# Inverse square roots of the norms: one power instruction on GpSimd in place of eleven Newton instructions on VectorE

## The chip, the cores and the metric

One core of a Trainium2 chip runs the whole program. The metric is device time in microseconds (us), taken as the median of repeated runs. The engines are called by the names of the profile: PE (TensorE, the matrix engine; PEld is its weight load), DVE (VectorE), ACT (ScalarE), POOL (GpSimd) and SP (SyncE, which issues the DMAs).

## What is computed

Two blocks of two layers each, over 512 tokens of width 1024, in float32. The first block mixes attention (with 256 context tokens beside the 512), a 31-wide depthwise convolution and a pooling branch, then a gated feed-forward part. The second block mixes a low-rank latent attention (MLA) with a gated linear attention (GLA) and adds a per-layer embedding. What matters here is that every norm needs the inverse square root of a mean over channels, one number per token and head:

```python
def rms_norm(t, g):
    ms = jnp.mean(jnp.square(tf), axis=-1, keepdims=True)
    return (tf * lax.rsqrt(ms + RMS_EPS)).astype(t.dtype) * g
def layer_norm(t, g, b):
    return ((tf - mu) * lax.rsqrt(var + LN_EPS)).astype(t.dtype) * g + b
```

## The kernel before, in words

Every matrix product is made of three: weights and activations are split into a high and a low part, and high x high, high x low and low x high are accumulated. Weights come in pieces of 128 x 1024 by SP's queue, ACT rounds a piece to the high part (line 178) and DVE subtracts to get the low part (line 181); nearly all PE work is `mm` (line 186).

No order of instructions is written out by hand for the engines. The program is written in source order, with priorities for some stretches, and a planner that simulates a timeline by its own costs orders each engine's instructions; each engine then runs its list in that order. The list mixes instructions of parts that do not depend on each other.

Forty inverse square roots are taken, all by `rsqrt` (lines 203 to 215). Tokens lie on the 128 partitions, so a root has only 2 to 12 columns. From a bit trick as the first guess (lines 209 and 210), three Newton rounds follow, of three DVE instructions each (lines 212, 213, 214): eleven small instructions, each of which needs the one before. The input is made on DVE by one affine instruction (mean and epsilon). The callers:

- `inv_rms` (20 roots): squares on ACT, column sums on PE, the sums turned onto the partitions by small products, then the affine line 264 out of PSUM, then `rsqrt`. It serves `ln` (the convolution's layer norm, and both layer norms of `out_ffn`, by segment), `norm_in` (the input norms of the second block, half the tokens at a time) and `final`. The result goes to PE, which multiplies it with the identity to broadcast it along the partitions (`bcast_cols`); what is scaled by the norm, on DVE or ACT, comes after.
- `kv` (4 roots, 6 columns): line 434, then `rsqrt`; ACT then scales the keys (line 439) before they are transposed.
- `qtrans` (8 roots, 8 or 12 columns): line 479, `rsqrt`, and line 482, which folds in the attention scale. Its result is used per query tile in `softmax`, by a small DVE multiply and by ACT's exponential.
- `lowrank_scale` (4 roots): lines 1194 to 1197 make the input, `rsqrt`, then a product (line 1200). The second of each pair is broadcast by PE for the keys of the MLA (line 1502 uses it).
- `gla` (4 roots, 8 columns): line 1466, `rsqrt`, then ACT (1472) and DVE (1474) scale the outputs before they are transposed.

Beside them on DVE: the 31 taps of the convolution (line 593) in the attention stages; the last affine lines of the norms (281, 283, 1019). On POOL: the rope's products and table multiplies (370, 388, 395, 397), the pooling windows and their edges (632 to 646), rescaling of the residual (808, 809, 1005, 1006, 1023, 1308), and the GLA's gate subtraction and fills (1342, 1354, 1355, 1361, 1368, 1391). The scratch tiles of the roots come from a ring of 24 of 16 columns.

Of the kernel before, what the change touches and what calls it, by code (L numbers as in the profile page):

```python
# [10 lines left out]
F32 = mybir.dt.float32  # L11
F32R = mybir.dt.float32r
I32 = mybir.dt.int32
U32 = mybir.dt.uint32
AF = mybir.ActivationFunctionType
ALU = mybir.AluOpType
# [4 lines left out]
P = 128  # L21
# [9 lines left out]
RMS_EPS = 1e-6  # L31
ALPHA = (2 * DEPTH) ** 0.25
WINDOWS = (2, 4, 8, 16)
ATTN_SCALE = 128 ** -0.5
# [25 lines left out]
class W:  # L60


    def __init__(self, pieces, kp, mc):
        self.pieces, self.kp, self.mc = pieces, kp, mc
# [13 lines left out]
class Net:  # L78
# [15 lines left out]
    def __init__(self, es, tc, a):  # L94
        self.es, self.tc, self.nc, self.a = es, tc, tc.nc, a
        nc = self.nc
        self.n_w, self.npt, self.nps = 0, 0, 0
        self.cst = es.enter_context(tc.tile_pool(name="cst", bufs=1))
        self.wp = es.enter_context(tc.tile_pool(name="wp", bufs=1))
        self.xp = es.enter_context(tc.tile_pool(name="xp", bufs=1))  # L100
        self.dr = es.enter_context(tc.tile_pool(name="dr", bufs=1, space=DRAM))
        self.uid = 0
        self.cols2 = []
        for l in range(DEPTH):
            t = self.cst.tile([P, NCOL2], F32, name=f"cols2{l}")
            nc.sync.dma_start(t, a["cols2"][l])
            self.cols2.append(t)
        self.fin = self.cst.tile([P, 8], F32, name="fin")
        nc.sync.dma_start(self.fin, a["final_norm"])
        c = self.cst  # L110
        self.ident = c.tile([P, P], F32, name="ident")
        make_identity(nc, self.ident)
        self.ones = c.tile([P, P], F32, name="ones")
        nc.vector.memset(self.ones, 1.0)
        self.cmean = c.tile([P, P], F32, name="cmean")
        nc.vector.memset(self.cmean, 1.0 / 32)

# [82 lines left out]
                self.mm(ps[:m1 - m0, c0:c0 + n], wl, xh[:, c0:c0 + n], False, last)  # L200


    def rsqrt(self, x, n, out=None):

        v = self.nc.vector
        i = self.S(n, I32)
        y = self.S(n) if out is None else out
        t = self.S(n)
        v.tensor_scalar(i, x.bitcast(I32), 1, None, op0=ALU.logical_shift_right)
        v.tensor_scalar(y.bitcast(I32), i, -1, 0x5F3759DF, op0=ALU.mult, op1=ALU.add)  # L210
        for _ in range(3):
            v.tensor_tensor(t, y, y, ALU.mult)  # L212
            v.scalar_tensor_tensor(t, t, -0.5, x, ALU.mult, ALU.mult)
            v.scalar_tensor_tensor(y, t, 1.5, y, ALU.add, ALU.mult)
        return y

    def bcast_cols(self, ps, r, nt):

        for t in range(nt):
            self.mm(ps[:, t * P:(t + 1) * P], r[:, t:t + 1].broadcast_to([P, P]), self.ident, True, True)  # L220
# [190 lines left out]
    def kv(self, l, j, toks, out):  # L411

        nc = self.nc
        tab = self.table(l, 1)
        w = self.wload(self.a["w_in"][l, CH_KV + j], KT, 256)
        brow = self.c1.tile([P, 256], F32, tag="brow", bufs=2, name=self.nm("brow"))
        nc.sync.dma_start(brow[:, :P], self.a["b_rows"][l:l + 1, 1024 + j * P:1024 + (j + 1) * P].broadcast_to([P, P]))
        vh, vl = self.al("KV", F32R), self.al("KV", F32R)
        kh, kl = self.al("KV", F32R), self.al("KV", F32R)
        ss = self.S(6)  # L420
        os = []
        for tp in range(3):
            ps = self.ps("pp")
            self.tok_proj(ps, w, *toks[tp])
            pv = ps[:, :512].rearrange("p (t h d) -> p t h d", t=2, h=2)
            vv = pv[:, :, 1, :]
            dst = slice(2 * tp * P, (2 * tp + 2) * P)
            hv = vh[:, dst].rearrange("p (t d) -> p t d", t=2)
            nc.scalar.copy(hv, vv)
            nc.vector.tensor_tensor(vl[:, dst].rearrange("p (t d) -> p t d", t=2), vv, hv.bitcast(F32), ALU.subtract)  # L430
            os.append(self.norm_rope(ps, pv[:, :, 0:1, :], brow[:, :P], 1, tp, tab, ss[:, 2 * tp:2 * tp + 2]))
            yield
        x = self.S(6)
        nc.vector.tensor_scalar(x, ss, 1.0 / 128, RMS_EPS, op0=ALU.mult, op1=ALU.add)
        r = self.rsqrt(x, 6)
        for tp in range(3):
            o = os[tp]
            for i in range(2):
                nc.scalar.activation(o[:, i * P:(i + 1) * P], o[:, i * P:(i + 1) * P], AF.Copy, scale=r[:, 2 * tp + i:2 * tp + i + 1])
            pt = self.ps("pt")  # L440
            for i in range(2):
                nc.tensor.transpose(pt[:, i * P:(i + 1) * P], o[:, i * P:(i + 1) * P], self.ident)
            self.split(kh[:, tp * 256:tp * 256 + 256], kl[:, tp * 256:tp * 256 + 256], pt[:, :256])
        out["kv", j] = kh, kl, vh, vl
        yield
# [18 lines left out]
    def qtrans(self, os, ss):  # L464

        nc = self.nc
        qs = []
        for o in os:
            pt = self.ps("pt")
            for t in range(2):  # L470
                for h in range(2):
                    nc.tensor.transpose(pt[:, h * 256 + t * P:h * 256 + (t + 1) * P],
                                        o[:, (t * 2 + h) * P:(t * 2 + h + 1) * P], self.ident)
            qh, ql = self.al("Q", F32R)[:, :SEQ], self.al("Q", F32R)[:, :SEQ]
            self.split(qh, ql, pt[:, :512])
            qs.append((qh, ql))
        n = 4 * len(os)
        x = self.S(12)
        nc.vector.tensor_scalar(x[:, :n], ss[:, :n], 1.0 / 128, RMS_EPS, op0=ALU.mult, op1=ALU.add)
        r = self.rsqrt(x[:, :n], n)  # L480
        sc = self.S(12)
        nc.vector.tensor_scalar(sc[:, :n], r, ATTN_SCALE, None, op0=ALU.mult)
        return qs, sc

    def softmax(self, ps, n, sc, out):

# [830 lines left out]
    def gla(self, l, j, q, k, sm, gv, md):  # L1317

        nc = self.nc
        v, s, g = nc.vector, nc.scalar, nc.gpsimd  # L1320
# [102 lines left out]
        ss = self.S(8)  # L1423
# [3 lines left out]
        for t in range(4):  # L1427
# [34 lines left out]
            s.copy(og[:, t * 256:(t + 1) * 256], po[:, :256])  # L1462
            for hh in range(2):
                s.activation(junk[:, :P], po[:, hh * P:(hh + 1) * P], AF.Square, accum_out=ss[:, 2 * t + hh:2 * t + hh + 1])
        x = self.S(8)
        v.tensor_scalar(x, ss, 1.0 / P, RMS_EPS, op0=ALU.mult, op1=ALU.add)
        r = self.rsqrt(x, 8)
        for hh in range(2):
            for t in range(4):
                o = og[:, t * 256 + hh * P:t * 256 + (hh + 1) * P]  # L1470
# [239 lines left out]
```

## Time and profile before

| what | value |
|---|---|
| median of 3 runs | 3476.34 us (3474.51 to 3477.19) |
| the profiled execution's own time | 3477.77 us |
| its span | 3476.0 us |
| mean granted TensorE clock | 0.961 |
| PE busy | 94% of the span |
| DVE busy | 64% |
| ACT busy | 40% |
| POOL busy | 15%, 581 instructions |

The profile shows one execution. Its span runs from the first to the last instruction; the execution's own time has a little around it. Busy time is that of the instructions alone, without the waiting before them. A line number is a line of the kernel; several callers can share the line of a helper such as 186 or 212. Where an instruction stood idle first, the profile names what ended the wait.

### The profile page before, as it was taken

What the parts mean: (1) busy time and instruction counts of PE and PEld (TensorE: products, weight loads), DVE (VectorE), ACT (ScalarE), POOL (GpSimd) and SP (SyncE); (2) the same over time, 40 slices, a digit from 0 to 9 for tenths busy, and PEclk for the clock granted to TensorE, in tenths of its full rate; (3) what the DMA queues carried; (4) which work ended last, traced back from release to release, by engine and by line L of the source; (5) the groups of instructions that cost most, each with busy time, mean ns of one, the idle gap of its engine ahead of it and who ended that gap; (6) DMA issues with size and microseconds to landing.
All of it is one profiled execution on the core that took longest, in us unless ns stands there. A gap on an engine that the chain in (4) does not pass through costs nothing.

```text
span 3476.0 us, 47198 instructions
## 1 busy us (share of the span) xinstructions
PE 3252.7 (94%) x18622; PEld 2680.6 (77%) x18622; DVE 2215.7 (64%) x3623; ACT 1381.4 (40%) x2362; POOL 528.7 (15%) x581
## 2 busy tenths in 40 slices
PE   7999999899999999999999989999998979998897
PEld 4887787778778888877888857788877757886586
DVE  5795968744554444457988956654555675657655
ACT  2434343433332112233544434432335545554453
POOL 2120212222120000003111204200001220112101
PEclk8999999999999999998999999999999989999899
DMA  6232312233333432232222234433333222442223
GB/s 250 67 117 88 120 56 70 68 98 93 102 122 128 140 122 64 58 106 82 76 66 85 88 99 131 122 96 97 97 115 107 90 68 85 148 155 86 79 87 108
DMA packets 110909, 350.80 MB, mean 101 GB/s; under 512 B 12832, under 2 KB 19424, under 8 KB 105568
## 3 DMA queue, kind: packets, MB, share of 16 engines
q1 hardware_dynamic: 110688, 347.79, 31.5%
q8 instruction: 146, 2.39, 0.3%
q14 instruction: 75, 0.61, 0.1%
HBM read 326.77 MB, written 20.97 MB: 100 GB/s over the span
## 4 chain that ended last, share of the span: by engine, by line
PE 71%; DVE 13%; ACT 3%; issue 2%; POOL 1%; DMA 0%; POOLq 0%; DVEq 0%; SPq 0%; ACTq 0%
PE pp L186 59%; DVE W L593 5%; PE st L186 3%; PE ps L186 3%; PE pv L186 2%; DVE wl L181 1%; PE pt L186 1%; DVE T L287 1%; DVE s L489 1%; ACT wh L178 0%; DVE M L287 0%; PE pt L527 0%; PE gb L1457 0%; DVE s L212 0%; ACT M L286 0%
## 5 line engine op out<-in xcount | busy, mean ns | idle before, releaser
L181 DVE TENSOR_TENSOR wl<-wr,wh 128x1024 fp32r<-128x1024 f32 (+2 forms) x482 | 589.5, 1226 | 353.7 <-ACT wh L178 351.5
L178 ACT CAST wh<-wr 128x1024 fp32r<-128x1024 f32 (+2 forms) x482 | 490.8, 1021 | 768.8 <-PE pp L186 701.1
L186 PE MATMUL pp<-A,wh 128*128 128x512 f32 (+1 forms) x3392 | 774.6, 343 | 17.8 <-ACT A L286 7.9
L186 PE MATMUL pp<-C,wh 128*128 128x512 f32 (+1 forms) x2328 | 658.5, 368 | 31.6 <-DVE M L1212 18.5
L186 PEld LDWEIGHTS pp<-A,wh 128*128 128x128 f32 x3392 | 537.7, 191 | 128.7 <-issue 25.1
L186 PEld LDWEIGHTS pp<-C,wh 128*128 128x128 f32 x2328 | 415.8, 192 | 123.0 <-issue 35.1
L186 PE MATMUL pp<-A,wl 128*128 128x512 f32 (+1 forms) x1696 | 460.4, 340 | 0.0
L186 PE MATMUL pp<-C,wl 128*128 128x512 f32 (+1 forms) x1164 | 424.9, 366 | 0.0
L186 PE MATMUL pp<-B,wh 128*128 128x512 f32 (+1 forms) x1296 | 315.9, 350 | 0.0
L186 PE MATMUL pp<-M,wh 128*128 128x256 f32 (+1 forms) x1280 | 293.8, 324 | 12.9 <-ACT M L1114 4.5
L186 PEld LDWEIGHTS pp<-A,wl 128*128 128x128 f32 x1696 | 271.9, 190 | 39.4 <-issue 4.7
L593 DVE SCALAR_TENSOR_TENSOR W<-W,cw,W 128x783 f32<-128x783 f32 x240 | 269.2, 1125 | 2.1
L186 PEld LDWEIGHTS pp<-C,wl 128*128 128x128 f32 x1164 | 223.0, 192 | 44.2 <-issue 8.6
L186 PEld LDWEIGHTS pp<-M,wh 128*128 128x128 f32 x1280 | 214.6, 194 | 43.3 <-issue 14.1
L186 PEld LDWEIGHTS pp<-B,wh 128*128 128x128 f32 x1296 | 212.1, 188 | 37.8 <-issue 2.9
L186 PE MATMUL pp<-M,wl 128*128 128x256 f32 (+1 forms) x640 | 205.8, 322 | 0.0
L186 PE MATMUL pp<-B,wl 128*128 128x512 f32 (+1 forms) x648 | 193.5, 349 | 0.0
L593 DVE SCALAR_TENSOR_TENSOR W<-U,cw,W 128x512 f32<-128x512 f32 x240 | 189.2, 789 | 3.0
L866 DVE SCALAR_TENSOR_TENSOR B<-pp,cols,B 128x511 f32<-128x511 f32 x66 | 43.4, 658 | 211.6 <-ACT B L863 211.4
L831 DVE SCALAR_TENSOR_TENSOR X<-pp,g,X 128x512 f32<-128x512 f32 (+1 forms) x128 | 76.9, 630 | 156.2 <-PE pp L186 155.9
L863 ACT ACTIVATE B<-pp,cols 128x768 f32<-128x768 f32 (+1 forms) x44 | 38.9, 885 | 232.9 <-PE pp L186 232.9
L186 PEld LDWEIGHTS pp<-M,wl 128*128 128x128 f32 x640 | 124.3, 194 | 9.2 <-issue 2.0
(398 smaller groups left out, 4938.5 us busy)
## 6 DMA issues: line engine op xcount, KB each, us to landing
wr<-w_in SPq DMA_DIRECT2D x184, 512.0 KB, 3.8
wr<-w_up SPq DMA_DIRECT2D x96, 512.0 KB, 3.8
wa<-w_ada SPq DMA_DIRECT2D x40, 1024.0 KB, 5.0
wr<-w_out SPq DMA_DIRECT2D x64, 512.0 KB, 3.9
wr<-w_down SPq DMA_DIRECT2D x48, 512.0 KB, 3.6
wr<-w_ple_gate SPq DMA_DIRECT2D x32, 512.0 KB, 4.1
Z<-w_ada SPq DMA_DIRECT2D x16, 512.0 KB, 8.5
wr<-conv_pw SPq DMA_DIRECT2D x16, 512.0 KB, 3.8
```

The costliest lines, as they stand in the source:

```text
L178: nc.scalar.copy(hi[:, :n], raw[:, :n])
L181: eng.tensor_tensor(lo[:, :n], raw[:, :n], hi[:, :n].bitcast(F32), ALU.subtract)
L186: self.nc.tensor.matmul(out, l, r, start=start, stop=stop)
L287: self.nc.vector.tensor_tensor(lo, t, hi.bitcast(F32), ALU.subtract)
L489: nc.vector.tensor_reduce(nm, ps[:, :n], AX.X, ALU.max, negate=True)
L593: nc.vector.scalar_tensor_tensor(y, gl[:, i:i + no], ws[:, i:i + 1], y, ALU.mult, ALU.add)
L831: nc.vector.scalar_tensor_tensor(xs[t][:, c0:c0 + sn], ps[:, c0:c0 + sn], g5[:, t, q:q + 1], xs[t][:, c0:c0 + sn], ALU.mult, ALU.add)
L863: nc.scalar.activation(y[:, :n], pa[:, :n], AF.Identity, bias=self.col(l, "fdw_b")[:, f:f + 1], scale=cw[:, 1:2])
L866: nc.vector.scalar_tensor_tensor(y[:, c0 + 1:e], pa[:, c0:e - 1], cw[:, 0:1], y[:, c0 + 1:e], ALU.mult, ALU.add)
```

## The change

`rsqrt` becomes one `tensor_tensor` power on POOL, with a constant tile of -0.5 as the exponent, and where a scale is asked for, one POOL multiply behind it. A new helper `rms_scale` also makes the input on POOL (mean and epsilon), for `kv`, `qtrans` and `gla`. `inv_rms` and `lowrank_scale` make their input on DVE as before and only the root moves. The constant is filled by DVE once, at the start.

```diff
--- before.py
+++ after.py
@@ -112,6 +112,8 @@
         make_identity(nc, self.ident)
         self.ones = c.tile([P, P], F32, name="ones")
         nc.vector.memset(self.ones, 1.0)
+        self.nhalf = c.tile([P, 16], F32, name="nhalf")
+        nc.vector.memset(self.nhalf, -0.5)
         self.cmean = c.tile([P, P], F32, name="cmean")
         nc.vector.memset(self.cmean, 1.0 / 32)
 
@@ -200,19 +202,19 @@
                 self.mm(ps[:m1 - m0, c0:c0 + n], wl, xh[:, c0:c0 + n], False, last)
 
 
-    def rsqrt(self, x, n, out=None):
-
-        v = self.nc.vector
-        i = self.S(n, I32)
+    def rsqrt(self, x, n, out=None, scale=1.0):
+
         y = self.S(n) if out is None else out
-        t = self.S(n)
-        v.tensor_scalar(i, x.bitcast(I32), 1, None, op0=ALU.logical_shift_right)
-        v.tensor_scalar(y.bitcast(I32), i, -1, 0x5F3759DF, op0=ALU.mult, op1=ALU.add)
-        for _ in range(3):
-            v.tensor_tensor(t, y, y, ALU.mult)
-            v.scalar_tensor_tensor(t, t, -0.5, x, ALU.mult, ALU.mult)
-            v.scalar_tensor_tensor(y, t, 1.5, y, ALU.add, ALU.mult)
+        self.nc.gpsimd.tensor_tensor(y, x, self.nhalf[:, :n], ALU.pow)
+        if scale != 1.0:
+            self.nc.gpsimd.tensor_scalar(y, y, scale, None, op0=ALU.mult)
         return y
+
+    def rms_scale(self, ss, n, d, scale=1.0):
+
+        x = self.S(n)
+        self.nc.gpsimd.tensor_scalar(x, ss[:, :n], 1.0 / d, RMS_EPS, op0=ALU.mult, op1=ALU.add)
+        return self.rsqrt(x, n, None, scale)
 
     def bcast_cols(self, ps, r, nt):
 
@@ -430,9 +432,7 @@
             nc.vector.tensor_tensor(vl[:, dst].rearrange("p (t d) -> p t d", t=2), vv, hv.bitcast(F32), ALU.subtract)
             os.append(self.norm_rope(ps, pv[:, :, 0:1, :], brow[:, :P], 1, tp, tab, ss[:, 2 * tp:2 * tp + 2]))
             yield
-        x = self.S(6)
-        nc.vector.tensor_scalar(x, ss, 1.0 / 128, RMS_EPS, op0=ALU.mult, op1=ALU.add)
-        r = self.rsqrt(x, 6)
+        r = self.rms_scale(ss, 6, 128)
         for tp in range(3):
             o = os[tp]
             for i in range(2):
@@ -475,12 +475,7 @@
             self.split(qh, ql, pt[:, :512])
             qs.append((qh, ql))
         n = 4 * len(os)
-        x = self.S(12)
-        nc.vector.tensor_scalar(x[:, :n], ss[:, :n], 1.0 / 128, RMS_EPS, op0=ALU.mult, op1=ALU.add)
-        r = self.rsqrt(x[:, :n], n)
-        sc = self.S(12)
-        nc.vector.tensor_scalar(sc[:, :n], r, ATTN_SCALE, None, op0=ALU.mult)
-        return qs, sc
+        return qs, self.rms_scale(ss, n, 128, ATTN_SCALE)
 
     def softmax(self, ps, n, sc, out):
 
@@ -1462,9 +1457,7 @@
             s.copy(og[:, t * 256:(t + 1) * 256], po[:, :256])
             for hh in range(2):
                 s.activation(junk[:, :P], po[:, hh * P:(hh + 1) * P], AF.Square, accum_out=ss[:, 2 * t + hh:2 * t + hh + 1])
-        x = self.S(8)
-        v.tensor_scalar(x, ss, 1.0 / P, RMS_EPS, op0=ALU.mult, op1=ALU.add)
-        r = self.rsqrt(x, 8)
+        r = self.rms_scale(ss, 8, P)
         for hh in range(2):
             for t in range(4):
                 o = og[:, t * 256 + hh * P:t * 256 + (hh + 1) * P]
```

## Rows read from the trace of the kernel before

**Rows 1.** The page: span; busy time, share of it and instructions of each engine.

```profile
span 3476.0 us, 47198 instructions
...
PE 3252.7 (94%) x18622; PEld 2680.6 (77%) x18622; DVE 2215.7 (64%) x3623; ACT 1381.4 (40%) x2362; POOL 528.7 (15%) x581
```

**Rows 2.** Stretch, its length; busy PE, PEld, DVE, ACT, POOL; PEclk, DMA, GB/s.

```profile
1600.00:1830.00 230.00, 219.75 (x1303) 192.04 (x1303) 202.00 (x344) 109.22 (x223) 38.02 (x46) 0.99 0.25 76
2785.00:2830.00 45.00, 29.22 (x127) 20.65 (x127) 36.98 (x77) 14.02 (x27) 19.14 (x19) 0.70 0.15 50
```

**Rows 3.** Line L212: count, ns (min/median/max), first and last start, shapes.

```profile
L212 DVE TENSOR_TENSOR s<-s x120: 149/161/1233, 92.0 to 3467.3; 128x2 f32<-128x2 f32 x48, 128x8 f32<-128x8 f32 x24, 128x4 f32<-128x4 f32 x21, 128x6 f32<-128x6 f32 x15
```

**Rows 4.** Timeline: start, us, engine, line, operation [idle before <- releaser].

```profile
968.63 0.16 DVE L264 TENSOR_SCALAR s<-st 128x2 f32<-128x2 f32 x1 [4.40 <-PE st L186]
...
970.79 0.16 DVE L214 SCALAR_TENSOR_TENSOR s<-s,s 128x2 f32<-128x2 f32 x1
...
971.10 0.55 PE L186 MATMUL st<-ident,s 128*128 128x128 f32 x1 [2.51 <-DVE s L214]
```

**Rows 5.** What PE waited for: us in total, times, the longest.

```profile
PE pt L186 <- DVE s L214: 11.0, 5, 2.8
PE st L186 <- DVE s L214: 10.9, 3, 4.7
```

**Rows 6.** Timeline of all engines, from three stretches with an exposed root.

```profile
1563.42 0.16 DVE L264 TENSOR_SCALAR s<-st 128x2 f32<-128x2 f32 x1 [3.21 <-PE st L186]
...
1568.53 0.58 PE L186 MATMUL pt<-ident,s 128*128 128x128 f32 x1 [2.82 <-DVE s L214]
...
2227.91 0.16 DVE L264 TENSOR_SCALAR s<-st 128x2 f32<-128x2 f32 x1 [3.33 <-PE st L186]
...
2231.52 0.55 PE L186 MATMUL st<-ident,s 128*128 128x128 f32 x1 [3.65 <-DVE s L214]
...
2610.99 0.16 DVE L264 TENSOR_SCALAR s<-st 128x2 f32<-128x2 f32 x1 [1.96 <-PE st L186]
...
2612.26 3.21 DVE L1019 SCALAR_TENSOR_TENSOR X<-X,cols,st 128x256 f32<-128x256 f32 x8
...
2616.65 1.23 PE L186 MATMUL st<-ident,s 128*128 128x128 f32 x4 [4.73 <-DVE s L214]
2617.99 0.48 DVE L1019 SCALAR_TENSOR_TENSOR X<-X,cols,st 128x256 f32<-128x256 f32 x1 [1.40 <-PE st L186]
```

**Rows 7.** POOL's groups by shape: busy us, mean ns | idle before.

```profile
L644 POOL TENSOR_TENSOR W<-W,edge 128x1 f32<-128x1 f32 x4 | 3.0, 772 | 0.0
...
L646 POOL TENSOR_TENSOR W<-W,edge 128x1 f32<-128x1 f32 x4 | 0.8, 192 | 0.0
```

**Rows 8.** Timeline, POOL's table multiplies beside a root's second step.

```profile
1563.20 3.70 POOL L370 TENSOR_TENSOR T<-T,grow 128x512 f32<-128x512 f32 x3 [0.86 <-DMA T<-rope_cos]
...
1564.52 1.19 DVE L210 TENSOR_SCALAR s<-s 128x2 int32<-128x2 int32 x1
```

**Rows 9.** Timeline of the gap in the first layer of block 2.

```profile
2787.70 0.34 DVE L1197 TENSOR_SCALAR s<-s 128x4 f32<-128x4 f32 x1
...
2788.04 0.52 POOL L1355 MEMSET G<- 64x512 f32 x1
...
2789.91 2.54 POOL L1342 TENSOR_TENSOR L<-L,G 128x512 f32<-128x512 f32 x2 [1.35 <-DVE L L1331]
...
2790.34 0.89 DVE L209 TENSOR_SCALAR s<-s 128x4 int32<-128x4 int32 x1
...
2807.94 0.16 DVE L1200 TENSOR_TENSOR s<-s,s 128x4 f32<-128x4 f32 x1
...
2808.25 0.55 PE L186 MATMUL pv<-ident,s 128*128 128x128 f32 x1 [3.15 <-DVE s L1384]
```

**Rows 10.** DVE's timeline in the second layer's attention: ends of one `qtrans` root.

```profile
1693.22 0.70 DVE L479 TENSOR_SCALAR s<-s 128x8 f32<-128x8 f32 x1
...
1711.45 0.16 DVE L482 TENSOR_SCALAR s<-s 128x8 f32<-128x8 f32 x1
```

## The prediction

> **What bounds the kernel now.** I read the page's busy shares first: TensorE (PE) is busy 3252.7 us of 3476.0, VectorE (DVE) 2215.7, GpSimd (POOL) only 528.7 [rows 1]. So the end moves only where PE stands still, or where another engine is saturated and PE starves behind it. The table by stretch shows where that is [rows 2]. In the attention of the second layer (1600 to 1830) DVE is busy 202.00 of 230.00 us. In the 45 us from 2785 DVE is busy 36.98 and PE only 29.22, at a mean granted clock of 0.70: a gap in which PE waits for a string of short steps.
>
> Next I read the Newton lines. L212 stands for all: three of it per root, 120 in all, so 40 roots; its median is 161 ns and its longest 1233 ns [rows 3]. By the code the 40 roots are 20 from `inv_rms`, 4 from `lowrank_scale`, 4 from `kv`, 8 from `qtrans` and 4 from `gla`. Where DVE has nothing else to do, a root looks like the one at 968 us [rows 4]: the input line L264 starts at 968.63, the last L214 starts at 970.79, and PE's broadcast of the root starts at 971.10, after standing 2.51 us. That is 2.47 us from input to consumer: eleven dependent steps 0.20 apart and a hop of about 0.15 to PE (970.79 + 0.16 to 971.10). The list of PE's waits shows how often it matters: L214 released PE eight times, for 11.0 and 10.9 us [rows 5]. Seven of the eight are long; the eighth, 0.5 us, is left at nothing.
>
> **Part one: the exposed roots.** Six more roots look like that one [rows 6]. The list pairs input and broadcast of 1563.42 and 1568.53, of 2227.91 and 2231.52, and of 2610.99 and 2616.65; the roots that enter at 3022.70, 3435.37 and 3465.55 repeat the 2.47 of [rows 4], PE standing 2.51, 2.71 and 2.51. With the change the path is L264 (0.16), a hop to POOL, the power, and a hop to PE. I take 0.2 for both hops, an estimate a little over the one of 0.15 above, and call the power p: p + 0.35 in place of 2.47.
>
> The trace has no power on POOL, so p is bounded by POOL's smallest multiplies: 0.19 us for a 128x1 one that met nothing, 0.77 for one that shared the time with DVE's convolution [rows 7]. The low end is 0.19. For the high end I let the power cost eleven of the dear multiplies, 8.5 us, as if POOL did Newton's work itself. I take p = 1.0: a power is more than one multiply, and the widths are 2 to 12 columns, so I go somewhat over the dear row it is nearest to.
>
> At p = 1.0 the path is 1.35. The four plain roots save 1.1 each, 4.4. The one at 2227.91 saves 3.61 - 1.35 = 2.3. For the one at 2610.99 the reader behind it (L1019 of the second segment, at 2617.99) comes after eight L1019 of the first segment (3.21 us from 2612.26), which end at 2615.5; it can't start earlier, so 2.5 is saved and not 4.3 [rows 6]. At 1563 POOL runs three table multiplies for 3.70 us from 1563.20 [rows 8]; the power stands before them or behind, so I take half of 5.11 - 1.35: 1.9. Sum: 11.1 us, and it falls by 7 for each us more of p.
>
> **Part two: the gap in each layer of the second block.** The second `lowrank_scale` enters DVE at 2787.70 and its product L1200 ends at 2808.10; PE's broadcast of it starts at 2808.25 after standing 3.15 us [rows 9] (the profile names L1384, a fill behind L1200, but the operand is L1200's). In between the planner has strewn the eleven steps among the GLA's work, and DVE never rests. The eleven add up to 4.56 us, since some last far over the median: the L209 takes 0.89 [rows 9], and the L212 at 2806.28 is the longest of all, 1.23 [rows 3]. All eleven become POOL's one instruction. POOL is free from the end of a fill at 2788.56 to the gate subtraction at 2789.91 [rows 9], so at p = 1.0 the power fits in front of it. If p is longer, that subtraction, the scan behind it on DVE and the whole GLA wait; that is the cover, and it costs p less 1.0 if gone. Saved: 3.5 a layer, leaving one for port waits; the second layer repeats it at 3196 to 3216. Sum 7.0, falling by 2 per us of p.
>
> **Part three: the twelve roots of the attention stages** (`kv` four times, `qtrans` eight). Here DVE's order mixes the steps with convolution taps: one `qtrans` root runs from 1693.22 to 1711.61 [rows 10]. Mixed so, a step costs DVE about 0.1 us, some 1.3 us a root with the two affine lines. In exchange POOL gets two instructions per `kv` root and three per `qtrans` root, 32 in all: the affine one, the power and the scale. At 0.75 for each small one and 1.0 for a power that is 4 x 1.75 + 8 x 2.5 = 27 us of POOL.
>
> How much of it stalls DVE is read from [rows 8]: an L210 of two columns that began beside POOL's three table multiplies lasted 1.19 us, about the length of one of the three, where a step takes 0.16 when POOL rests [rows 4]. So a DVE step can wait for a whole POOL instruction. Not every DVE line will meet one, so I take half of the 27 as stalls: 12 x 1.3 - 13.5 = +2, of which I book nothing, as the attention doesn't end on DVE alone. The bounds are +16 (no stall) and 16 - 27 = -11 (all of it). Per us of p it loses 12 x 0.5 = 6.
>
> [...]
>
> Behind a waiting affine line on POOL stand the rope multiplies and the pooling windows; who waits for the result is ScalarE's scaling of the keys and, new, the softmax's small multiply on DVE.
>
> **Part four, at nothing.** The other roots, thirteen of `inv_rms` and the first of each `lowrank_scale` pair, have PE's other products beside them: [rows 5] has no wait for them. If that cover were gone each would cost or save its own p + 0.35 against 2.47. The four roots of the GLA outputs feed ScalarE and DVE ahead of the transposes, and release PE nowhere in [rows 5]. The constant is one DVE fill before the first L212 at 92.0 us [rows 3]. Fewer scratch tiles rotate; no DMA is added or moved, so SP's queue has nothing new ahead of it.
>
> **Sum.** 11.1 + 7.0 + 0 = 18 us. The profiled execution took 3477.77, its span 3476.0 with 1.8 around it, 1.4 above the median of 3476.34. Taken off the median: 3458. The rate over all parts is 7 + 2 + 6 = 15 us per us of p, so the gain is gone at p = 2.2.
>
> [...]
>
> **Rivals.** First, **slower: the power is dear.** [...] It decides at p = 2.2. At p = 3 the time is 3476 + 12 = 3488, at 4 us 3503, at the bound of 8.5 us 3571. For it: POOL does nothing like a power here, and its 128x1 multiply can take 0.77. Against it: three multiplies of 512 columns take POOL 3.70 us together [rows 8], and here there are 12 columns at most. Chance 0.21.
>
> [...] Chance 0.07.
>
> Third, **the gain is given back.** Behind an exposed root comes ScalarE's copy or split and then weights that wait anyway, and the planner orders every engine anew, with shifts of a few us either way. For it: the root at 2610.99, half covered by L1019. Against: PE has no matmul between input and broadcast in the seven. Time 3472 to 3480. Chance 0.09.
>
> Fourth, **the change does not do what it says**: the power is queued behind long POOL work, so that a wait for POOL takes the place of eleven steps. Time about 3476; chance 0.03, since of the seven only the one at 1563 has POOL work between input and broadcast.
>
> **How the numbers follow.** Forecast 0.60, rivals 0.21, 0.07, 0.09 and 0.03. What a measurement can tell from no change is about 0.2%, 7 us: 3469 to 3483. The forecast lies below that (p under 1.5), the first rival above, the others within or at its edge: faster 0.60, same 0.19, slower 0.21. The predicted time is the forecast's, 3458. The range's low end is p = 0.19: 18 + 15 x 0.8 = 30 us, 3446. The high end is the first rival at p = 3, 3488; what is beyond, up to 3571, and a re-plan better than the low end hold less than 0.2.
>
> **What would show it.** Right: a POOL power of about 1 us; 1.3 us from L264 to the broadcast at the seven places; no long Newton line in the gap, and that gap 3 to 4 us shorter; DVE less busy by the 440 steps, some 70 us at their median. Wrong: powers over 2.2 us, convolution taps (L593) longer than before beside them, PE's waits moved from L214 to POOL at the same length, or a time that falls outside the places named.

## The result: 3438 us, and the profile after

The changed kernel takes **3438.45 us** (median of 4 runs, 3434.70 to 3442.10), the kernel before beside it 3475.43 (4 runs): a ratio of 0.9898, 95% interval 0.9879 to 0.9917. The direction was forecast, the size was not: 18 us were predicted and 35.5 came (1.02% of 3475), and 3438 lies below the range of 3446 to 3488. The profiled execution took 3437.51.

The page of the kernel after, its span and its busy times by engine, to set against [rows 1]:

```profile
span 3435.7 us, 46787 instructions
...
PE 3238.6 (94%) x18622; PEld 2670.4 (78%) x18622; DVE 2152.9 (63%) x3160; ACT 1380.5 (40%) x2362; POOL 597.1 (17%) x645
```

DVE lost 463 instructions but only 62.8 us; POOL gained 64 and 68.4 us. PE runs the same 18622 matmuls in 14 us less at a higher granted clock (0.967 over the span, 0.961 before); between the second profiles named below it is 6 us (0.967 and 0.964).

The powers, from the table of POOL's groups by shape (busy us, mean ns of one | idle before):

```profile
L208 POOL TENSOR_TENSOR s<-s,nhalf 128x8 f32<-128x8 f32 x8 | 15.4, 1924 | 0.4
...
L208 POOL TENSOR_TENSOR s<-s,nhalf 128x2 f32<-128x2 f32 x16 | 11.4, 712 | 602.0 <-DVE s L266 602.0
...
L208 POOL TENSOR_TENSOR s<-s,nhalf 128x12 f32<-128x12 f32 x4 | 10.8, 2698 | 0.3
```

A power costs 0.71 us at 2 columns, 1.92 at 8 and 2.70 at 12 in the mean; the 40 together take 54.7 us, 1.37 each. The exposed roots are of 2 columns. Here is the one that [rows 4] shows before, in the timeline of all engines:

```profile
953.98 0.16 DVE L266 TENSOR_SCALAR s<-st 128x2 f32<-128x2 f32 x1 [4.42 <-PE st L188]
954.22 0.70 POOL L208 TENSOR_TENSOR s<-s,nhalf 128x2 f32<-128x2 f32 x1 [7.05 <-DVE s L266]
...
954.98 0.71 PE L188 MATMUL st<-ident,s 128*128 128x128 f32 x4 [1.04 <-POOL s L208]
```

Input to consumer is 1.00 us where it was 2.47: 0.16 for the affine line, 0.08 to POOL, 0.70 for the power, 0.06 to PE. The list of PE's waits (us in total, times, longest) answers to [rows 5]:

```profile
PE pt L188 <- POOL s L208: 4.3, 4, 1.2
...
PE st L188 <- POOL s L208: 2.1, 2, 1.0
```

21.9 us of standing in front of the roots became 6.4. Not all of it came off the time: part turned up in the next wait, as the part on the prediction shows.

**Two profiles of each kernel.** Both kernels were profiled once more, unaltered (runs r_before_again and r_after_again, below). Before, the spans were 3476.0 and 3465.0; after, 3435.7 and 3430.3. One program thus differs by 11 us from one execution to the next, and a term of that size can't be read off a single pair. I compare the second profile of each (34.7 us apart) by the starts of the same root's input line (L264 before, L266 after), and say where the first pair differs:

```
                                          before          after          saved
start to conv-LN root, layer 0 attention  0 - 748.2       0 - 736.8      11.4
to the root once at 964                   964.3           951.7           1.1
to the root once at 1559                  1559.1          1545.3          1.3
to the middle of layer 1's softmaxes      1734.9          1717.7          3.4
to the end of that attention              2078.3          2059.0          2.1
to the root once at 2596                  2596.0          2573.9          2.8
to the root once at 2635                  2635.1          2606.0          7.0
to the first lowrank root of layer 0      2775.7          2747.7         -1.1
GLA gap, layer 0 (to the first output)    2826.7          2797.3          1.3
rest of GLA and MLA, layer 0              2959.8          2934.3         -3.8
to the first lowrank root of layer 1      3178.0          3150.9          1.6
GLA gap, layer 1                          3228.7          3200.3          1.3
rest of GLA and MLA, layer 1              3369.9          3337.3          4.2
to the end                                3461.5          3426.8          2.1
```

Grouped: the attention stages 13.5 (11.4 + 2.1), the GLA gaps 2.6, the stages right behind the gaps 0.4, all other stretches 18.2. The first profile of after gives 8.7 instead of 11.4 in the first line and 29.3 in all. Of the 3.4 in the fourth line, 2.8 lie ahead of layer 1's first softmax and come also in e1 below, which has Newton in that attention: they are the root once at 1559.

### The profile page after: what moved, and what is told of

The parts are those of the page before. It is cut to its first block, busy times and chain, and to the rows that moved or that the text cites. A ratio compares the mean times of both kernels' runs of the same rounds, so it can differ in the third digit from the quotient of the medians.

```text
span 3435.7 us, 46787 instructions
## 1 busy us (share of the span) xinstructions
PE 3238.6 (94%) x18622; PEld 2670.4 (78%) x18622; DVE 2152.9 (63%) x3160; ACT 1380.5 (40%) x2362; POOL 597.1 (17%) x645
## 4 chain that ended last, share of the span: by engine, by line
PE 71%; DVE 11%; ACT 3%; issue 2%; DMA 1%; POOL 1%; SPq 0%; POOLq 0%; DVEq 0%; ACTq 0%
PE pp L188 60%; DVE W L588 4%; PE st L188 3%; PE ps L188 3%; PE pv L188 2%; DVE wl L183 1%; PE pt L188 1%; DVE T L289 1%; ACT wh L180 1%; DVE s L484 0%; PE pt L522 0%; DMA yd<-W 0%; DVE M L289 0%; DVE M L1207 0%; PE ga L188 0%
## 5 line engine op out<-in xcount | busy, mean ns | idle before, releaser
L208 POOL TENSOR_TENSOR s<-s,nhalf 128x2 f32<-128x2 f32 (+4 forms) x40 | 54.6, 1366 | 1335.5 <-DVE s L266 1331.8
```

Of the source, the lines that this page charges most:

```text
L208: self.nc.gpsimd.tensor_tensor(y, x, self.nhalf[:, :n], ALU.pow)
```

## The experiments

Ratios are to the kernel before on the same chip. "Port" in the prediction and the expectations stands for what was read from [rows 8]: a DVE step that lasted 1.19 us beside POOL's work, where one took 0.16 with POOL at rest [rows 4]. What makes such a step long, no run shows.

**e1_attention_newton** puts Newton back into `kv` and `qtrans`, on DVE with its affine and scale lines:

```diff
-        r = self.rms_scale(ss, 6, 128)
+        r = self.rms_scale_newton(ss, 6, 128)
...
-        return qs, self.rms_scale(ss, n, 128, ATTN_SCALE)
+        return qs, self.rms_scale_newton(ss, n, 128, ATTN_SCALE)
```

> Newton on DVE again for the twelve roots of kv and qtrans, the power for the other 28. Theory A (the attention's gain is DVE time: the steps stood in a stretch that ends on DVE, and the power on POOL does not give it back through the port): about 17 of the 37 us come back, 3455 us. Rival B (the twelve roots cost nothing there, and the attention got shorter because the planner happened on a better order): no fixed relation; near 3438 if the steps are free.

**e2_attention_power** is its complement: the power in those twelve roots alone.

```diff
-        return self.rsqrt(x, nt, out)
+        return self.rsqrt_newton(x, nt, out)
...
-        y = self.rsqrt(x, 4)
+        y = self.rsqrt_newton(x, 4)
...
-        r = self.rms_scale(ss, 8, P)
+        r = self.rms_scale_newton(ss, 8, P)
```

> The complement: the power for the twelve roots of kv and qtrans alone, Newton on DVE for inv_rms, lowrank_scale and gla. Theory A: 17 us under the kernel before, 3458, and the two halves add up to the whole. Rival B: near 3475, or halves that do not add up to 37 us within some 6 us.

Measured: e1 3445.0 us (0.992, 0.9907 to 0.9932), e2 3453.0 (0.9943, 0.9929 to 0.9957). So the attention's roots alone bring 20 us by the ratio, where the prediction booked none; taken out of the change they cost 8 (it keeps 28). The two halves add up to more than the whole (28 + 20 against 35.5), so their sizes are not clean terms; the place is. The conv-LN root at the end of layer 0's attention starts between 736.8 and 740.4 in every run with the power in `kv` and `qtrans` (after twice, e2, e3, e7, e8), at 746.4 to 752.7 in every run with three Newton rounds there, and at 756.5 with six (e6). At that root the two swaps agree: 9.6 us (e1 against r_after_again) and 9.2 (e2 against r_before_again). The stretch from 100 us to that root, columns as in [rows 2], in the order before again, after again, e1, e2:

```profile
100.00:748.23 648.23, 609.68 (x3773) 519.89 (x3770) 485.28 (x701) 262.59 (x509) 122.31 (x135) 0.97 0.27 86
100.00:736.82 636.82, 604.59 (x3760) 516.03 (x3760) 475.15 (x632) 258.66 (x499) 140.07 (x149) 0.98 0.27 88
100.00:746.37 646.37, 608.98 (x3761) 519.02 (x3760) 484.45 (x699) 261.44 (x507) 122.51 (x135) 0.97 0.26 86
100.00:739.02 639.02, 606.80 (x3757) 517.99 (x3757) 475.54 (x630) 258.72 (x499) 139.62 (x149) 0.97 0.27 87
```

PE stands (the length less its busy time) 38.6 and 37.4 us with Newton in the attention, 32.2 and 32.2 with the power. Over all profiles it is 36.2 to 41.5 with three rounds, 45.4 with six, and 31.3 to 34.3 with the power.

Layer 1 hardly takes part. From the root once at 1559 to the one that ends its attention, e1 takes 514.4 us with DVE busy 419.9, r_after_again 513.7 with 405.5; the other swap, e2 against r_before_again, is 2.7 us of time for 11 of DVE.

How layer 0 gains shows in the stretch between two softmaxes that bracket the densest part of its attention. Table by stretch; columns as in [rows 2]. Before, second profile:

```profile
324.70:451.20 126.50, 119.37 (x774) 103.59 (x775) 115.71 (x159) 42.88 (x97) 37.28 (x45) 0.99 0.34 109
```

After, second profile:

```profile
319.70:442.80 123.10, 119.03 (x774) 103.84 (x775) 111.88 (x135) 43.07 (x97) 43.81 (x50) 0.99 0.34 112
```

The same 774 matmuls at the same clock; DVE has 24 instructions and 3.8 us less, POOL 6.5 us more, and the stretch is 3.4 us shorter, as PE stands 4.1 us in place of 7.1. That less DVE work is what shortens it is likely here and not shown: in layer 1 much more off DVE brought less. POOL's 6.5 us, half of which the prediction charged to DVE, left no mark.

**e7_attention_thrice** tests that charge: each of the twelve attention powers is executed three times.

```diff
-        return self.rsqrt(x, n, None, scale)
+        y = self.S(n)
+        if d == 128 and n != 8 or scale != 1.0:
+            for _ in range(2):
+                self.nc.gpsimd.tensor_tensor(y, x, self.nhalf[:, :n], ALU.pow)
+        return self.rsqrt(x, n, y, scale)
```

> The changed kernel with the power issued three times in the twelve roots of kv and qtrans: 24 more powers of 1.63 to 2.70 us, 53 us of POOL. If half of POOL's length stops DVE, as the prediction had it: 26 us slower than the changed kernel, 3465. Rival (the attention does not feel POOL's small instructions): under 5 us, 3438 to 3443.

Measured: 3441.3 us (0.9923, 0.9910 to 0.9936), span 3437.6. POOL's busy time rose by 49.2 us to 646.3, and the same stretch reads:

```profile
319.90:445.10 125.20, 120.78 (x774) 105.03 (x775) 111.86 (x134) 43.05 (x97) 51.91 (x54) 0.97 0.34 110
```

Eight us more of POOL than after, and DVE's busy time is the same to 0.02 us. Of the 2.1 us that the stretch lost, 1.8 are PE's busy time at a clock of 0.97 in place of 0.99. The 480 convolution taps tell the same over the whole run: 466.4 us in e7, 465.6 after, 458.4 before. The change itself cost them 7 us; 49 us more of powers, one. Laid tap by tap against POOL's timeline, e7 shows why. A tap beside a power and nothing else on POOL takes 1.03 us (783 columns, 18 of them) or 0.75 (512 columns, 14), the same as beside an idle POOL. Nearly all of the 7 us lies in the taps beside POOL's other `tensor_tensor` instructions, 1.41 us (783 columns) and 1.03 (512) in the mean after, 1.34 and 0.99 before. What gives way is the power: of 6 columns it takes 1.33 to 1.35 us with no tap beside it, 2.0 to 2.1 beside taps of 1.02 and 1.03 (after). By the medians and by the ratios e7 is 3 to 9 us above the changed kernel, where half of 49 would be 25. All of it, the case of part three's lower bound of -11 us, would be 49; beside the powers the taps show no such cost (1.03 us with and without).

**e3_power_twice** executes every power twice, one behind the other.

```diff
         self.nc.gpsimd.tensor_tensor(y, x, self.nhalf[:, :n], ALU.pow)
+        self.nc.gpsimd.tensor_tensor(y, x, self.nhalf[:, :n], ALU.pow)
```

> [...] By the prediction's slopes (7 exposed roots at 0.71, two gaps at 1.27, half of the attention's 12 powers, 26 us, as DVE stalls): 5 + 2.5 + 13 = 20 us over the changed kernel, 3459. Rival (the port costs the attention next to nothing, its powers are hidden): 7 us, 3446.

Measured: 3457.2 us (0.9957, 0.9945 to 0.9969), 20 us above the change by the ratios, for 1.37 us more per root: 15 us per us of p, the rate that the prediction gave. The path of an exposed root became 1.77 us. But the rate comes about in another way. At the seven exposed roots together e3 loses 4.5 us against r_after_again and in the two gaps 2.2, about as the prediction's slopes have it; in layer 0's attention, where they put most of the rest, PE stands 32.4 us (32.2 in r_after_again). Span less PE's busy time is 197.8 us against 197.1 in the first profile of after and 192.1 in the second, while its busy time is up by 22.6 and 23.0, at a mean clock of 0.958 in place of 0.967. In the two MLA stretches shown under e8 alone, e3 takes 12.6 us more than r_after_again, at 0.87 and 0.89 in place of 0.96.

**e4_newton_urgent** keeps Newton and gives its eleven steps a higher priority in the planner.

```diff
+    rprio = 1000
...
-        v.tensor_scalar(i, x.bitcast(I32), 1, None, op0=ALU.logical_shift_right)
...
+        with self.tc.high_priority(offset=self.rprio):
+            v.tensor_scalar(i, x.bitcast(I32), 1, None, op0=ALU.logical_shift_right)
...
```

> The kernel before with the eleven steps at a raised priority in the planner, so that DVE runs them close together instead of strewn among other work; DVE does the same work. Theory A (DVE time counts): only the strewn exposed roots and the gaps gain, some 5 us, 3470. Rival C (it is the lateness of a strewn root that holds up what follows, in the attention too): most of the gain of the attention comes without POOL, 3455.

Measured: 3468.4 us (0.9989, 0.9978 to 1.0001), no change that can be told. But the edit did not do what it was made for: from a root's first step to its last, the forty take 273.7 us together, in r_before_again 273.9, and the longest, in layer 0's attention, 22.89 us in both. The steps are as strewn as before, so the run says nothing on rival C, that the lateness of a strewn root costs the time and not its steps. Two things speak against C in the attention: between 100 and 748 us of r_before_again no wait of PE ends with a root's step or with the scaling of the keys (L439), and in e7 two more powers make each of the twelve roots later by some 3 to 6 us, while PE stands 31.8 us there (32.2 and 34.3 after). Neither excludes it, since the Newton roots there were up to 23 us long.

**e6_six_rounds** lengthens Newton from three rounds to six, nine steps more per root.

```diff
-        for _ in range(3):
+        for _ in range(6):
```

> The kernel before with six Newton rounds, so nine more small DVE steps in each of the 40 roots. By the prediction's prices: 7 x 9 x 0.2 = 12.6 at the exposed roots, 2 x 9/11 x 4.56 = 7.5 in the gaps, 12 x 9 x 0.1 = 11 at most in the attention: 20 to 31 us slower, 3493 to 3504. Theory A adds half as much again for the clock: 3503 to 3519, and PE's busy time grows though it has the same matmuls.

Measured: 3529.3 us (1.0173, 1.0159 to 1.0187), 60 us for nine steps, 6.7 for one step in 40 roots, and more than either theory said. Against r_before_again, PE's waits on L214 rose from 21.6 to 37.1, those at the gaps' broadcast from 6.6 to 14.0, and PE's busy time by 36 us at a clock of 0.951.

**e5_inv_rms_only** leaves the power in the 20 roots of `inv_rms` alone.

```diff
-        y = self.rsqrt(x, 4)
+        y = self.rsqrt_newton(x, 4)
...
-        r = self.rms_scale(ss, 6, 128)
+        r = self.rms_scale_newton(ss, 6, 128)
...
-        return qs, self.rms_scale(ss, n, 128, ATTN_SCALE)
+        return qs, self.rms_scale_newton(ss, n, 128, ATTN_SCALE)
...
-        r = self.rms_scale(ss, 8, P)
+        r = self.rms_scale_newton(ss, 8, P)
```

> The power for the twenty roots of inv_rms alone; Newton on DVE for kv, qtrans, lowrank_scale and gla. Theory A (PE's waits for these roots fell by 15.5 us, and with every us that PE does not stand about half a us of its own busy time goes too, since less of it runs at the lower clock): 15.5 + 8 = 23 us under the kernel before, 3449. Rival (no return of the clock): 15.5, 3457.

Measured: 3459.3 us (12 runs, 3448.15 to 3467.60; 0.9978, 0.9966 to 0.9989). Median and profile don't agree: the profiled execution took 3448.15, the fastest of the twelve. Its profile saves 18.6 us against the second one of before; the median of 12 runs saves 8 to 9. That the 20 roots gain is shown, by how much is not.

**r_before_again and r_after_again** are the two kernels unaltered, the first as a single execution.

> The kernel before, unchanged, for a second profile of it: how far two executions of the same instructions differ by stretch. Its first profile took 3477.8, five above the median of 17 runs. If that sits in the first layer's attention, the lead of 13 us that the changed kernel's profile has there at 740 us is smaller by it.

Measured: 3466.8 us, span 3465.0.

> The changed kernel once more, unaltered, for the spread of one program and for the comparison with the kernel beside it. Both theories: 3438 us, 3432 to 3445; the profiled execution within 5 us of the first one (span 3435.7), the difference in TensorE's busy time and not in the places of the roots. If it stands 10 us off, single profiles can't settle terms under that size.

Measured: 3434.2 us (4 runs; 0.9897, 0.9876 to 0.9918), span 3430.3.

**e8_gla_newton** takes the power out of `lowrank_scale` and the GLA output alone.

```diff
-        y = self.rsqrt(x, 4)
+        y = self.rsqrt_newton(x, 4)
...
-        r = self.rms_scale(ss, 8, P)
+        r = self.rms_scale_newton(ss, 8, P)
```

> The changed kernel with Newton again in the four lowrank_scale roots and the four GLA output roots; the power stays in the other 32 roots. Theory A (the gap of the GLA, which the prediction put at 7 us, gives nothing net): within 3 us of the changed kernel, so 3435 to 3441; from the first lowrank root to the output root of layer 0 of the second block 184 us in place of 188, in layer 1 about 324 in place of 321; 7 us from the first to the second lowrank root in place of 11. Rival (the prediction's 7 us are there): 7 us slower than the changed kernel, about 3445, both gaps 3 to 4 us longer.

Measured: 3446.2 us (0.9930, 0.9914 to 0.9945), 12 us slower than r_after_again on the same chip. By the total theory A falls, but the rival's place is wrong too. The gap isn't where the 12 us are: from the first lowrank root to the first GLA output e8 takes 50.7 and 50.8 us, the changed kernel 49.7 and 49.4. Only 2.4 of the 12 lie there. PE's waits in layer 0's gap say why. Before, second profile:

```profile
PE pp L186 <- DVE M L1212: 7.3, 1, 7.3
PE pv L186 <- DVE s L1384: 3.4, 1, 3.4
PE gb L1401 <- POOL L L1391: 1.6, 1, 1.6
...
PE pp L186 <- DVE M L1502: 0.9, 1, 0.9
```

After, second profile:

```profile
PE pp L188 <- DVE M L1207: 7.0, 1, 7.0
PE pp L188 <- DVE M L1495: 3.2, 1, 3.2
PE gb L1396 <- POOL L L1386: 1.6, 1, 1.6
```

The wait for the root's broadcast, 3.4 us, is gone, as the prediction had it. The next product to be late waits for the key's scaling by that broadcast (`kn`, L1502 before, L1495 after): 0.9 became 3.2. DVE gets to it behind the scan L1340 (1.21 us) and a split (L289, 1.46), large steps that the wait for the root had hidden.

Of the rest, 3.7 us lie ahead of the first root that differs, 1.5 and 1.6 in the two stretches behind the gaps (14.7 to 16.3 us with 70 matmuls, at a clock of 1.00 and 0.90), and 2.8 and 2.6 in the two from there to the next root of `norm_in` (MLA). These hold the same 624 to 626 matmuls in every kernel, and their length goes by the granted clock, the last column but two. Layer 0, from four profiles: before,

```profile
2846.21:2971.33 125.12, 114.58 (x626) 88.02 (x625) 75.13 (x150) 72.51 (x131) 6.55 (x6) 0.92 0.30 101
```

before again,

```profile
2841.35:2959.80 118.45, 105.87 (x626) 82.43 (x625) 75.16 (x151) 72.35 (x131) 6.54 (x6) 1.00 0.32 107
```

after again,

```profile
2812.12:2934.31 122.19, 110.16 (x624) 85.23 (x623) 73.23 (x138) 72.71 (x131) 8.38 (x8) 0.96 0.30 103
```

and e3:

```profile
2823.32:2953.03 129.71, 119.78 (x624) 91.45 (x623) 73.94 (x139) 72.96 (x131) 10.66 (x9) 0.87 0.29 97
```

At 1.00 throughout, the stretch takes 118 us; at a mean of 0.87, 130. In the first of the four, at a mean of 0.92, the granted clock is 0.50 from 2896 to 2909 and 1.00 from 2910 to the end. It is no matter of the roots' form alone: e2, with Newton there, takes 118.3 in layer 0, and e1, with the power, 118.6 in layer 1, both at 1.00. The gap ahead, where PE stands about a third of the time (14.7 of 49.7 us in r_after_again), differs by at most 2 us between these runs, and what comes behind it by up to 11. Why one execution of before was granted 1.00 there and another 0.92 stays open.

## Why the direction was right and the size wrong

**Part three, the attention, is the step that failed.** It set stalls against a saving and booked nothing; 13.5 us came off in the two attention stages, 11.4 of them in layer 0 (by the swaps of e1 and e2, 9.6 and 9.2 in layer 0 and 0.7 and 2.7 in layer 1). What failed is "so I take half of the 27 as stalls", a rule made from one L210 that lasted 1.19 us beside POOL's table multiplies [rows 8]. The 27 us of POOL were near: e1, which takes them out, has 31 to 33 less. A small DVE step was long beside a wide POOL instruction again (an L1191 took 1.25 us beside L1337 in r_after_again), but the taps are as short beside the powers as without (1.03 us, e7). The saving was too small as well: for 12 x 1.3 = 16 us, e1 has DVE busy 22 to 23 us more than the changed kernel. The reason for booking nothing, that "the attention doesn't end on DVE alone", failed in layer 0 and nearly held in layer 1; the sum had no term that told the layers apart. And the range forgot this bound: its low end took p = 0.19 but left out the +16 that the part itself named as the case without stalls. 3476 - 18 - 16 = 3442 belonged in it.

**Part one, 11.1 us, was too small by p and by one root.** The mechanism was right at all seven places and p was close (0.71, 1.0 taken). With p = 0.70 its own rate gives 13.2. From each root's input line to PE's first product behind the broadcast (for the last root, to the end), the seven places took 49.6 us before and 35.4 after, in both pairs of profiles: 14.2 saved. The covers that it booked were there. At 2611 the wait of 4.73 [rows 6] went, but PE's next wait, for the first piece that the second block reads (L1114 before, L1109 after), grew from 4.33 to 6.68; from input to that product 2.8 us were saved, where 2.5 were booked. At 1563 the wait of 2.82 went and the next one, for ACT, grew from 0.19 to 1.36: 2.0 saved (1.6 in the second pair), 1.9 booked. That the booked half came out is luck: the power got in front of the table multiplies (it starts at 1547.71, they at 1548.54), and it was the next wait that took the other half. The eighth root, "left at nothing", was not nothing: its path of 5.92 us, strewn among DVE's other work, became 1.57, and the stretch from the product behind the root at 2611 to the next root's input gained 3.7 us. 14.2 and 3.7 make 17.9, near the 18.2 that all stretches outside attention and gaps gained, though single ones went either way (2.8, -1.1, 1.6).

**Part two, 7.0, was too large in its place:** 1.3 us a layer, not 3.5. The prediction asked what would be late next for the POOL subtraction and not for PE's next product; the answer was `kn`, behind the scan. The us a layer that it left for port waits is shown by no run; what the runs show in its place is that the wait for the broadcast, 3.4 us, went and the one for `kn` grew from 0.9 to 3.2. In e8 the total lost 12 us without this part, of which 2.4 lie in the gaps; the 8.5 behind them go with the clock, and 3.7 are there ahead of the first root that differs, so the runs don't say what this part is worth beyond its gaps.

**The sum.** Booked 11.1 + 7.0 + 0 = 18; read from the pair of second profiles 18.2 + 2.6 + 13.5 + 0.4 = 34.7, against 35.5 by the ratio.

**The rivals.** The dear power (0.21) fell: it decides at p = 2.2, and the mean of 40 is 1.37, the exposed ones 0.71. The bound from POOL's 128x1 multiply at 0.77 [rows 7] was the better guide. The one of 0.07, with part three at its lower bound of -11, fell with e7's taps (1.03 us beside a power and without). Given back (0.09) shows in one place, -1.1; the -3.8 goes with the clock of 1.00 in before again (against the first profile of before, that stage saves 1.5 in the first of after). The fourth (0.03) fell at the waits: 6.4 us in place of 21.9.

Of what was to be seen: 1.3 us from L266 to the broadcast (1.00), gaps 3 to 4 us shorter (1.3), DVE 70 us less busy (63), taps longer (by 1.5%, without deciding).

## What to carry to other kernels

A string of dependent small instructions can cost its latency where somebody waits (2.47 us at an exposed root here, 1.00 with the power) and its engine's time where that engine is full (likely here in layer 0's attention alone); price both, place by place. What a us off a full engine is worth can't be taken for granted: 3.8 us off DVE went with 3.4 off one stretch, and 11 to 14 us off with 0.7 to 2.7 off the next layer's attention. The risk on the other engine needs a row for its bulk instructions, not for one small step. When a wait goes, read what PE waits for next before the saving is booked. When bounds are named, put the good one into the range as well as the bad one. And look in the trace whether an edit moved what it was to move, as e4's did not.

## Not expected of the hardware

A power on POOL grew with the columns: the shortest of each width took 0.69 us at 2, 1.01 at 4, 1.33 at 6, 1.64 at 8 and 2.27 at 12 (after), 0.16 for each. Beside DVE's taps the power got longer (6 columns: 2.0 to 2.1 in place of 1.33 to 1.35) and the taps did not (1.03). The same program ran 11 us apart, 6.7 of it in one MLA stage at a clock of 0.92 or 1.00. And doubling the powers added little to PE's standing time (197.8 us in place of 197.1 and 192.1): 22.6 and 23.0 us came as busy time, the same 18622 matmuls at a mean clock of 0.958 in place of 0.967. Why the chip grants less there, the runs don't show.
